# The low-rank gate of the third mixer: its first factor taken out of the weight stream

## The chip, the core and the metric

The kernel runs on one core of one Trainium2 chip. The metric is the device time of one launch in microseconds (us), lower is better. Three runs of the kernel before took 1793.9, 1794.4 and 1795.85 us; their median is 1794.4 us. A change of more than 0.2% (3.6 us) is about what a measurement of this kernel can tell from no change.

## What is computed

One layer of a hybrid decoder for 256 prompt tokens and 8 sampled tokens (264 columns together), everything in float32. One input projection `w_in` feeds three mixers; their outputs are projected, merged with gates, projected again, and an MLP follows. The part that the change touches is the third mixer (GLA), whose decay comes from a low-rank product: 2048 activations are first reduced to 16 numbers (`glr`) and then expanded to 512.

```python
h = rmsnorm(x, g_pre_mix) * (1.0 + sc1) + sh1
z = h @ w_in                       # 2048 x 15376
(z_uv, hq, hf, hi, hg, gq, gk, gv, gr, glr, z_gate) = split(z, offsets)
...
log_a = log_sigmoid(glr @ gla_w_up + gla_b_up) / GLA_TAU   # glr: 16 wide
o_g, S_g = gated_linear_recurrence(gq, gk * scale, gv, log_a, s_gla)
y_c = head_rmsnorm(o_g, gla_norm_g) * silu(gr)
merged = sum(gates[n] * (y_n @ w_branch[n]) for the three mixers)
out = merged @ w_out
```

## The kernel before

**The weight stream.** Almost all of the time goes into products of a weight matrix with the 264 activation columns. The activations are kept as two halves, `hh` and `hl` (a rounded part and the rest, blocks of [128, 4, 264]), and every weight is split in the same way: SP loads a raw item of [128 x 1024], ScalarE (ACT) casts each of its two halves to `whi` (`half_hi`, L667), VectorE (DVE) subtracts to get `wlo` (L671). One item makes one granule of 24 matmuls of 264 columns: for each 128 x 128 tile `whi` with `hh`, `whi` with `hl` and `wlo` with `hh`. `plan` lists the items in the order in which the granules come; items are loaded five ahead and split two ahead of the granule that uses them. `linear` and `zin` run the granules of one output tile and call `background()` after each.

**What runs beside it.** `background()` counts granules in `now` and advances the generators `mixer_a` and `mixer_r` (the three mixers) by a set rate per granule. These emit their small matmuls and transposes between granules, on PSUM tiles `sm` (three buffers), with their element-wise work on ACT and DVE. Some steps are held until a granule has passed (`READY`). `slot()` emits the matmuls of recurrence levels and of sampled states together with steps of the modulation weights (`ada`, float32, four groups of 32 columns of the array, L89, `Rounds.steps`).

**What sets the order.** In this part of the program the orders of PE and POOL are written out by hand: the instructions stand as the Python code emits them. ACT and DVE are given their work in the order that the scheduler of the language makes of it; each engine runs its list strictly in order.

**Where a mixer must be done.** The three branch products follow one another. At the start of the second (`branch(1, ...)`), `parts_b` calls `finish(0)` and `finish(1)`; `finish` calls `bg.drain`, which emits whatever is left of the mixer's generator at once, with no granule between. The last steps of a mixer are: eight matmuls for the outputs (`att`, L89), copies and squares on ACT (L1380, L1383), a reciprocal root on DVE (`rstd_small`, L249 to L255), eight scalings on ACT (L1389), and two sets of four transposes with their copies (L1400).

**The low-rank part.** `gla_group` allocates a block `wl`, zeroes it on POOL (L1141), loads the second factor `gla_w_up` into rows 0 to 15 of its first 512 columns (L1142), and runs `zin` over the columns of q and k. Then `z = zin(9216, P)` streams the first factor as an item 128 columns wide, of which 16 are used (two granules, 48 matmuls), and L1150 copies 16 rows of the sum to `lr`. After each tile of v one matmul with `wup` and `lr` gives 128 rows of the gate.

Of the kernel before, what the change touches and what calls it, by code (L numbers as in the profile page):

```python
# [7 lines left out]
F32 = mybir.dt.float32  # L8
# [7 lines left out]
P = 128  # L16
D = 2048
KT = D // P
NP = 256
NS = 8  # L20
NT = NP + NS
# [48 lines left out]
def hybrid_step_kernel(  # L70
# [8 lines left out]
    nc = tc.nc  # L79
    V, S = nc.vector, nc.scalar  # L80
# [23 lines left out]
    T = Products()  # L104
# [13 lines left out]
    def nm(s):  # L118
        uid[0] += 1
        return f"{s}_{uid[0]}"  # L120

    def blk(shape=None, dt=F32):
        shape = shape or [P, 4, NT]
        return blkp.tile(shape, dt, tag="b", name=nm("b"))

    def sm(shape=None):
        return psm.tile(shape or [P, 512], F32, tag="sm", name=nm("sm"))
# [10 lines left out]
    def add(o, a, b):  # L138
        V.tensor_tensor(o, a, b, op=ALU.add)  # L139
# [14 lines left out]
    def moving(v):  # L154
        return v.rearrange("p (r c) -> p c r", r=2)
# [43 lines left out]
    ps = sm()  # L199
# [121 lines left out]
    ps = sm([P, P])  # L321
# [184 lines left out]
    hh, hl = [], []  # L506
# [85 lines left out]
    def blocks(w, k0, nk, c0, width=CW):  # L592
        kc = min(nk, 1024 // width)
        return [(w, k0 + kb, kc, c0, width) for kb in range(0, nk, kc)]

    def plan():

        out, k0 = [], 0
        for n in CHUNKS:
            for gi in range(0, len(begin), 4 // n):  # L600
                out.append((win, k0, n, begin[gi][0], 4 // n * CW))
            k0 += n
        for c0 in (6144, 6400, 6656, 6912):
            out += blocks(win, 0, KT, c0)
        out += blocks(win, 0, KT, 9216, P)
        for s in range(4):
            out += blocks(win, 0, KT, 7168 + s * CW)
        for n in range(N_BRANCH):
            if n:
                g0 = 5120 if n == 1 else 8192  # L610
                for s in range(4):
                    out += blocks(win, 0, KT, g0 + s * CW)
            for m in range(8):
                out += blocks(win, 0, KT, 9232 + n * D + m * CW) + blocks(w_branch[0, n], 0, 8, m * CW)
        for m in range(8):
            out += blocks(w_out[0], 0, KT, m * CW)
        gap_at.append(len(out))
        for f in range(NFB + 1):
            if f < NFB:
                if f == 0:  # L620
                    out += blocks(w_mlp_up[0], 0, KT, 0, 2 * CW)
                for m in range(0 if f else 2, FB // CW):
                    out += blocks(w_mlp_up[0], 0, KT, f * FB + m * CW)
            if f:
                for m in range(8):
                    out += blocks(w_mlp_down[0], (f - 1) * (FB // P), FB // P, m * CW)
        return out
# [113 lines left out]
    def slot():  # L741

        lv = [x for x in levels if x[0] + AGE <= now[0]][:2]
        sv = [x for x in samples if x[0] + AGE <= now[0]]
        late = max([now[0] - x[0] for x in lv] + [0]) >= AGE + SLOT_WAIT + 3
        while lv and not T.room(LEVEL_N * len(lv) + 16 * len(sv)) and (len(lv) == 2 or not late):
            lv.pop()
        if lv or sv:
            T.short = T.spread(LEVEL_N * len(lv) + 16 * len(sv))
        del levels[:len(lv)]  # L750
        del samples[:len(sv)]
        if lv:
            pl = sm([P, 2, 8, 32])
            for i, (_, lhs, rhs, _) in enumerate(lv):
                for h in range(4):
                    for hf in range(2):
                        for b in range(4):
                            t0 = hf * P + b * 32
                            T.matmul(pl[32 * b:32 * b + 32, i, 2 * h + hf, :], lhs[:, h, t0:t0 + 32], rhs[:, h, t0:t0 + 32], start=True, stop=True)
        if sv:  # L760
            G, qm, os_ = sv[0][1]
            nh = 512 // G.dv
            po = sm([P, G.dv])
            for h in range(4):
                for i, (_, _, b, sts) in enumerate(sv):
                    T.matmul(po[32 * h:32 * h + 32, :], qm[:, h, b, :], sts[h // nh][:, h % nh, :], start=i == 0, stop=i == len(sv) - 1)
        if rounds.due():
            rounds.steps()
        for i, (_, _, _, put) in enumerate(lv):
            put(pl[:, i])  # L770
        if sv:
            if sv[0][2] == 0:
                V.tensor_copy(os_, po)
            else:
                add(os_, os_, po)
# [24 lines left out]
    def linear(w, k0, nk, c0, width, xh, xl):  # L800

        acc = new_acc()
        kc = min(nk, 1024 // width)
        for kb in range(0, nk, kc):
            granule(w, k0, kc, c0, width, [acc], xh, xl, kb, kb == 0, kb + kc == nk)
            background()
        return acc[:, 0:width // P, 0:NT]
# [4 lines left out]
    def pair(b, g):  # L812
        return b[:, 2 * g:2 * g + 2, :]
# [7 lines left out]
    win = w_in[0]  # L821

    def zin(c0, width=CW):
        return linear(win, 0, KT, c0, width, hH, hL)
# [26 lines left out]
    ]  # L851
    gap_at = []
    stream.append(Stream(plan()))
    stream[0].half_at = gap_at[0]
    first = First(0, CHUNKS[0])
# [224 lines left out]
    def log_sigmoid(out, z, a):  # L1080

        S.activation(a, z, AF.Abs)
        yield
        S.activation(a, a, AF.Exp, scale=-1.0)
        yield 1.6
        S.activation(a, a, AF.Ln, bias=1.0)
        yield 1.8
        V.scalar_tensor_tensor(out, z, 0.0, a, ALU.min, ALU.subtract)
        yield
# [45 lines left out]
    def gla_group():  # L1135
        G = Group()
        G.dv, G.i = 256, 2
        G.q, G.g, G.k, G.v = blk(), blk(), blk(), [blk(), blk()]
        wl = blk([P, 512 + NT])
        wup, lr = wl[:, 0:512], wl[:, 512:512 + NT]  # L1140
        nc.gpsimd.memset(wl, 0.0)  # L1141
        nc.gpsimd.dma_start(wup[0:16], gla_w_up[0])  # L1142
        for s in range(2):
            z = zin(6144 + s * CW)
            S.copy(pair(G.q, s), z)
        for s in range(2):
            z = zin(6656 + s * CW)
            S.activation(pair(G.k, s), z, AF.Copy, scale=GLA_SCALE)
        z = zin(9216, P)
        S.copy(lr[0:16], z[0:16, 0, :])  # L1150
        for s in range(4):
            z = zin(7168 + s * CW)
            S.copy(pair(G.v[s // 2], s % 2), z)
            ps = sm()
            T.matmul(ps[:, 0:NT], wup[:, s * P:(s + 1) * P], lr, start=True, stop=True)
            V.tensor_scalar(G.g[:, s, :], ps[:, 0:NT], bupT[:, s:s + 1], None, ALU.add)
        G.s_in = lambda b, h, n: state_gla[0, b, h:h + n].rearrange("h k v -> k h v")
        G.s_out = lambda b, h, n: gla_sample[0, b, h:h + n].rearrange("h k v -> k h v")
        G.p_out = lambda h, n: gla_prompt[0, 0, h:h + n].rearrange("h k v -> k h v")

        def gates():
            yield from log_sigmoid(G.g, G.g, blk())
            V.tensor_scalar(G.g, G.g, 1.0 / GLA_TAU, None, ALU.mult)
            yield

        G.gates = gates
        return G
# [251 lines left out]
    rate[:] = RATES[0]  # L1419
    rounds.gap = 2  # L1420
    Gs.append(gla_group())
    gens.append(mixer_r(Gs[2]))
    bg.g.append(gens[2])
# [162 lines left out]
    for m in range(8):  # L1586
# [4 lines left out]
        z = linear(w_out[0], 0, KT, m * CW, CW, mH, mL)  # L1591
# [37 lines left out]
    ps = sm([P, 2, KT, NS])  # L1629
# [197 lines left out]
    pt, ps = sm([P, 2, CW]), sm([P, 2 + NS])  # L1827
# [20 lines left out]
    def put(eng, t, hf, c0):  # L1848
        eng.dma_start(y_prompt[0, t * P:(t + 1) * P, hf * 1024 + c0:hf * 1024 + c0 + 512], piece(yt, t, hf, c0))
# [16 lines left out]
    ps = sm([P, P])  # L1866
# [63 lines left out]
```

## Time and profile before

| what | value |
|---|---|
| three runs | 1793.9, 1794.4, 1795.85 us |
| the profiled execution, its span | 1792.8 us (no time of its own is given beside it; the median of the runs is 1.6 us above) |
| busy: weight loads of PE, DVE, ACT, POOL | 94%, 66%, 56%, 8% |
| read from HBM | 427.60 MB, 245 GB/s over the span with what is written |
| the q tiles of the third mixer are copied (L1145) | 298.2 and 309.5 us |
| the low-rank sum is copied (L1150) | 347.2 us |

The span is the time from the first to the last instruction of one profiled execution. PE is the matmul engine; its weight loads overlap its matmuls and are listed as PEld. The chain of the profile is the work that ended last, followed back from the last instruction; a matmul group in it carries its time on PE. Matmuls are pipelined, so the duration of a single one (277 ns for a 264-column one) is longer than the distance from one to the next. A float32 matmul of the program stands in the trace as two records.

### The profile page before, as it was taken

To read this page: it belongs to the slowest core of one execution; us is meant where nothing else is said; L and a number is where in the kernel's file an instruction comes from. 1 tells how busy PE (TensorE), PEld (TensorE's weight loads), DVE (VectorE), ACT (ScalarE), POOL (GpSimd) and SP (SyncE) were. 2 spreads that over 40 slices of the span, in tenths; PEclk is the share of its full clock that TensorE was granted. 3 is DMA by queue.
4 is the path that set the end of the run, shared out by engine and by line. 5 is a ranking of instruction groups with operands and counts; after the bars stand their busy time and mean duration, and the time that the engine had idled before them with its cause. 6 is when DMAs were issued, how large, how long until landed. Compare 5 with 4: busy or idle time off the path is not lost.

```text
span 1792.8 us, 42113 instructions
## 1 busy us (share of the span) xinstructions
PE 1770.3 (99%) x16970; PEld 1686.2 (94%) x16970; DVE 1183.8 (66%) x2079; ACT 1002.5 (56%) x1823; POOL 140.5 (8%) x228
## 2 busy tenths in 40 slices
PE   6999999999999999999999999999999999999998
PEld 5899999989999999899999989999999999999997
DVE  5676668697588697466566666645666666666666
ACT  5444554666766766655455665555454545454544
POOL 4222000101102012110000010000000000000000
PEclk9999999999999999999999999999999999999999
DMA  9998597789699789898866946776666666666663
GB/s 343 392 354 296 184 340 249 227 293 309 208 290 320 236 285 311 286 370 264 266 193 206 319 140 220 239 254 204 193 196 198 194 197 195 194 199 192 198 191 117
DMA packets 330179, 442.05 MB, mean 247 GB/s; under 512 B 14946, under 2 KB 276944, under 8 KB 329984
## 3 DMA queue, kind: packets, MB, share of 16 engines
q1 hardware_dynamic: 312160, 381.05, 65.5%
q0 software_dynamic: 17184, 57.85, 9.2%
q8 instruction: 133, 2.18, 0.5%
q14 instruction: 62, 0.51, 0.1%
q10 hardware_dynamic: 640, 0.47, 0.1%
HBM read 427.60 MB, written 11.70 MB: 245 GB/s over the span
## 4 chain that ended last, share of the span: by engine, by line
PE 95%; DMA 2%; DVE 2%; ACT 1%; issue 0%; SPq 0%; DVEq 0%; ACTq 0%
PE mm L89 86%; PE ada L89 5%; PE sm L89 3%; PE sm L93 1%; DMA b<-in_w_ada_dram 1%; DVE wlo L671 1%; DMA b<-in_x_prompt_dram 0%; DVE b L139 0%; DVE b L1670 0%; DVE b L142 0%; ACT b L1356 0%; ACT b L145 0%; SPq L532 0%; SPq L186 0%; DVE b L136 0%
## 5 line engine op out<-in xcount | busy, mean ns | idle before, releaser
L89 PE MATMUL mm<-b,whi 128*128 128x264 f32 x9248 | 1578.8, 277 | 1.3 <-DVE b L920 0.4
L89 PEld LDWEIGHTS mm<-b,whi 128*128 128x128 f32 x9248 | 1394.4, 189 | 35.0 <-issue 19.9
L89 PE MATMUL mm<-b,wlo 128*128 128x264 f32 x4624 | 1275.5, 276 | 0.0
L671 DVE TENSOR_TENSOR wlo<-raw,whi 128x512 fp32r<-128x512 f32 x1118 | 760.3, 690 | 462.1 <-ACT whi L667 459.2
L667 ACT CAST whi<-raw 128x512 fp32r<-128x512 f32 x1118 | 681.7, 617 | 620.2 <-DVE wlo L671 315.6
L89 PEld LDWEIGHTS mm<-b,wlo 128*128 128x128 f32 x4624 | 873.5, 189 | 0.2
L139 DVE TENSOR_TENSOR b<-b,mm 128x528 f32<-128x528 f32 (+1 forms) x137 | 95.7, 699 | 55.6 <-PE mm L89 49.0
L89 PE MATMUL ada<-b,cT 128*32 128x256 f32 (+2 forms) x888 | 66.2, 421 | 3.4 <-DMA b<-in_w_ada_dram 3.1
L89 PEld LDWEIGHTS ada<-b,cT 128*32 128x32 f32 x888 | 26.1, 112 | 34.1 <-issue 17.2
L1860 POOL TENSOR_TENSOR gs<-b,G 128x16 f32<-128x16 f32 x1 | 0.2, 222 | 714.1 <-DVE b L139 714.1
L532 POOL DMA_DIRECT2D b<-in_w_ada_dram x64 | 46.3, 726 | 44.1 <-PE ada L89 35.1
L1214 POOL DMA_DIRECT2D out_dram<-st x32 | 23.5, 735 | 234.0 <-DVE st L1213 227.6
L667 ACT CAST whi<-araw 128x512 fp32r<-128x512 f32 x38 | 23.1, 618 | 26.2 <-PE mm L89 22.0
L89 PE MATMUL ada<-araw,cT 128*32 128x512 f32 x264 | 35.6, 599 | 0.0
L1211 ACT ACTIVATE st<-st,fs 128x128 f32<-128x128 f32 (+1 forms) x96 | 35.2, 426 | 0.0
L136 DVE TENSOR_TENSOR b<-b,b 128x512 f32<-128x512 f32 (+1 forms) x47 | 34.4, 747 | 1.2 <-ACT b L1325 0.8
L1213 DVE SCALAR_TENSOR_TENSOR st<-vbc,b,st 128x128 f32<-128x128 f32 (+1 forms) x96 | 32.4, 392 | 1.2 <-ACT st L1211 1.2
L93 PE MATMUL sm<-cst,b 128*128 128x128 f32 (+1 forms) x149 | 21.5, 285 | 8.2 <-DMA b<-in_g_post_mix_dram 5.0
L671 DVE TENSOR_TENSOR wlo<-araw,whi 128x512 fp32r<-128x512 f32 x38 | 24.6, 686 | 5.3 <-ACT whi L667 5.3
L93 PEld LDWEIGHTS sm<-cst,b 128*128 128x128 f32 (+1 forms) x149 | 17.5, 147 | 9.2 <-issue 6.0
L142 DVE TENSOR_TENSOR b<-b 128x1024 f32<-128x1024 f32 (+1 forms) x24 | 24.4, 1022 | 1.5 <-PE ada L89 1.4
L142 DVE TENSOR_TENSOR b<-gt,b 128x528 fp32r<-128x528 f32 x32 | 22.7, 709 | 3.6 <-ACT whi L667 0.5
(303 smaller groups left out, 819.5 us busy)
## 6 DMA issues: line engine op xcount, KB each, us to landing
raw<-in_w_in_dram SPq DMA_DIRECT2D x225, 512.0 KB, 5.2
raw<-in_w_mlp_down_dram SPq DMA_DIRECT2D x128, 512.0 KB, 3.6
raw<-in_w_mlp_up_dram SPq DMA_DIRECT2D x125, 512.0 KB, 3.9
araw<-in_w_ada_dram SPq DMA_DIRECT2D x66, 512.0 KB, 6.1
b<-in_w_ada_dram SPq DMA_DIRECT2D x62, 512.0 KB, 6.8
b<-in_w_ada_dram POOLq DMA_DIRECT2D x48, 512.0 KB, 9.6
raw<-in_w_branch_dram SPq DMA_DIRECT2D x48, 512.0 KB, 4.7
raw<-in_w_out_dram SPq DMA_DIRECT2D x32, 512.0 KB, 4.5
```

What stands on the lines that cost most here:

```text
L89: return nc.tensor.matmul(out, w, x, **kw)
L93: return nc.tensor.transpose(*a)
L136: V.tensor_tensor(o, a, b, op=ALU.mult)
L139: V.tensor_tensor(o, a, b, op=ALU.add)
L142: V.tensor_tensor(o, a, b, op=ALU.subtract)
L532: queue.dma_start(w[:, i], w1[k * P:(k + 1) * P, :, self.k0 * P:(self.k0 + self.n) * P])
L667: self.last = [S.copy(hi, raw).ins, None]
L671: self.last[1] = V.tensor_tensor(lo, raw, hi.bitcast(F32), op=ALU.subtract).ins
L1211: S.activation(st[:, i, :], st[:, i, :], AF.Copy, scale=fs[:, h0 + i, b:b + 1])
L1213: V.scalar_tensor_tensor(st[:, i, :], v[:, i, :], k[:, h0 + i, NP + b:NP + b + 1], st[:, i, :], ALU.mult, ALU.add)
L1214: nc.gpsimd.dma_start(G.s_out(b, h0, nh), st)
L1860: Q.tensor_tensor(gs[:, 14:16, :], dst[:, :, NP:NT], G2[:, 14:16, 1:NC], op=ALU.mult)
```

## The change

The first factor is no longer an item of the stream: the line in `plan` goes, and with it two items, their loads, four casts, four subtractions, two granules and their two calls of `background()`. Its 16 columns are loaded once by a POOL DMA straight into the second half of `wl`, as [128, 16, 32] with 16 of every 32 columns filled, and `gla_w_up` is loaded four times, at rows 0, 32, 64 and 96. A new function `low_rank` calls `slot()` and then emits 32 float32 matmuls of 32 x 264: for each block of four k tiles, and for both halves of the activations, four matmuls on four groups of 32 columns of the array. Their sums lie in four groups of 32 rows of one `sm` tile; they are copied whole (128 rows) to `lr`, which is now the last quarter of `G.g`, and the second product adds the four groups up by its contraction over 128 rows.

```diff
@@ plan
-        out += blocks(win, 0, KT, 9216, P)
@@ gla_group
-        wl = blk([P, 512 + NT])
-        wup, lr = wl[:, 0:512], wl[:, 512:512 + NT]
+        wl = blk([P, 1024])
+        wup, wlr = wl[:, 0:512], wl[:, 512:1024].rearrange("p (k c) -> p k c", k=KT)
         nc.gpsimd.memset(wl, 0.0)
-        nc.gpsimd.dma_start(wup[0:16], gla_w_up[0])
+        nc.gpsimd.dma_start(wlr[:, :, 0:16], win[:, 9216:9232].rearrange("(k p) c -> p k c", p=P))
+        for j in range(4):
+            nc.gpsimd.dma_start(wup[32 * j:32 * j + 16], gla_w_up[0])
+        lr = G.g[:, 3, :]
+
+        def low_rank():
+
+            slot()
+            ps = sm()
+            for s in range(4):
+                for i, x in enumerate((hh, hl)):
+                    for j in range(4):
+                        T.matmul(ps[32 * j:32 * j + 32, 0:NT], wlr[:, 4 * s + j, :], moving(x[s].bitcast(F32)[:, j, :]),
+                                 start=s == 0 and i == 0, stop=s == 3 and i == 1)
+            S.copy(lr, ps[:, 0:NT])
...
-        z = zin(9216, P)
-        S.copy(lr[0:16], z[0:16, 0, :])
+        low_rank()
```

**First place: PE at the low-rank product.** `mm` are the tiles of the stream, `sm` the small tiles; the two sets of transposes belong to the first HGRN mixer. Before, PE goes on with the stream (mm_4635 is the low-rank tile):

```order
L89 MATMUL mm_4454<-b_2720,wlo_4484 128x264
L93 MATMUL sm_4620<-cst,b_178 128x128 x4
L93 MATMUL sm_4627<-cst,b_178 128x128 x4
L89 MATMUL mm_4635<-b_331,whi_4521 128x264
L89 MATMUL mm_4635<-b_332,whi_4521 128x264
```

and with the change:

```order
L93 MATMUL sm_4624<-cst,b_178 128x128 x4
L93 MATMUL sm_4631<-cst,b_178 128x128 x4
L89 MATMUL sm_4639<-b_331,b_3876 32x264 x4
L89 MATMUL sm_4639<-b_332,b_3876 32x264 x4
L89 MATMUL sm_4639<-b_1254,b_3876 32x264 x4
L89 MATMUL sm_4639<-b_1255,b_3876 32x264 x4
L89 MATMUL sm_4639<-b_1993,b_3876 32x264 x4
L89 MATMUL sm_4639<-b_1994,b_3876 32x264 x4
L89 MATMUL sm_4639<-b_2720,b_3876 32x264 x4
L89 MATMUL sm_4639<-b_2721,b_3876 32x264 x4
L89 MATMUL mm_4673<-b_331,whi_4525 128x264
```

The 48 stream matmuls of the low-rank tile are gone, and 32 float32 matmuls stand directly behind the transposes; the next tile of the stream is the first v tile.

**Second place: PE and ACT at the start of the second branch.** The tiles `os` hold the sampled outputs of the two HGRN mixers; the transposes of b_8563 (before) or b_8631 (now) are the last ones of the second HGRN mixer. Before, they stand 96 stream matmuls (mm_8637) behind the mixer's last output products:

```order
L89 MATMUL mm_8637<-b_2720,wlo_8667 128x264
L93 MATMUL sm_8819<-cst,b_8563 128x128 x4
L93 MATMUL sm_8825<-cst,b_8563 128x128 x4
L93 MATMUL sm_8833<-cst,b_3874 128x128 x4
L93 MATMUL sm_8840<-cst,os_915_5285 128x128
L93 MATMUL sm_8844<-cst,os_1247_7431 128x128
L89 MATMUL mm_8856<-b_331,whi_8701 128x264
```

Now they stand 48 (the second half of mm_8576) behind them, and after the first `os` transpose, that is in the drain of `finish(1)`:

```order
L89 MATMUL mm_8576<-b_2720,wlo_8606 128x264
L93 MATMUL sm_8789<-cst,os_915_5354 128x128
L93 MATMUL sm_8798<-cst,b_8631 128x128 x4
L93 MATMUL sm_8804<-cst,b_8631 128x128 x4
L93 MATMUL sm_8810<-cst,os_1243_7436 128x128
L89 MATMUL mm_8822<-b_331,whi_8669 128x264
```

On ACT the eight scalings (L1389 before, L1402 now) that these transposes read stood, before, ahead of four casts and of the activation of the gate tile mm_8637:

```order
L1389 ACTIVATE b_8563<-b_8563,rr_8561 128x128 x2
L667 CAST whi_8705<-raw_8541 128x512
L1389 ACTIVATE b_8563<-b_8563,rr_8561 128x128 x2
L667 CAST whi_8770<-raw_8601 128x512
L667 CAST whi_8774<-raw_8601 128x512
L667 CAST whi_8808<-raw_8670 128x512
L667 CAST whi_8812<-raw_8670 128x512
L1468 ACTIVATE b_8020<-mm_8637 128x528
L1400 COPY b_8818<-sm_8819 128x2x256
```

Now the last four stand behind the activation of that gate tile (mm_8576), with the copy of the transposes next:

```order
L666 CAST whi_8760<-raw_8609 128x512
L1402 ACTIVATE b_8631<-b_8631,rr_8629 128x128 x3
L666 CAST whi_8764<-raw_8609 128x512
L1402 ACTIVATE b_8631<-b_8631,rr_8629 128x128
L1481 ACTIVATE b_7972<-mm_8576 128x528
L1402 ACTIVATE b_8631<-b_8631,rr_8629 128x128 x4
L1413 COPY b_8797<-sm_8798 128x2x256
```

Two granules of cover between the mixer's last products and its transposes are gone, the two that the low-rank tile had.

**Third place: POOL ahead of the third mixer's tiles.** Before:

```order
L480 TENSOR_TENSOR b_533<-xsn_132,A_169 128x2x8
L481 TENSOR_TENSOR b_533<-b_533,mod 128x2x8
L1141 MEMSET b_3876 128x776
L1142 DMA b_3876<-in_gla_w_up_dram 16x512
L1051 DMA out_dram<-sqs_4425 64x128
```

and now:

```order
L480 TENSOR_TENSOR b_533<-xsn_132,A_169 128x2x8
L481 TENSOR_TENSOR b_533<-b_533,mod 128x2x8
L1140 MEMSET b_3876 128x1024
L1141 DMA b_3876<-in_w_in_dram 128x16x16
L1143 DMA b_3876<-in_gla_w_up_dram 16x512 x4
L1050 DMA out_dram<-sqs_4429 64x128
```

POOL issues five DMAs where it issued one, and the first of them gathers 2048 pieces of 16 numbers (64 bytes).

## The prediction

> **What bounds the kernel now.** I read the page first, then the waits of PE, then single stretches of the timeline where the change acts.
>
> ```profile
> span 1792.8 us, 42113 instructions
> PE 1770.3 (99%) x16970; PEld 1686.2 (94%) x16970; DVE 1183.8 (66%) x2079; ACT 1002.5 (56%) x1823; POOL 140.5 (8%) x228
> PEclk9999999999999999999999999999999999999999
> PE 95%; DMA 2%; DVE 2%; ACT 1%; issue 0%; SPq 0%; DVEq 0%; ACTq 0%
> PE mm L89 86%; PE ada L89 5%; PE sm L89 3%; PE sm L93 1%; DMA b<-in_w_ada_dram 1%; DVE wlo L671 1%; DMA b<-in_x_prompt_dram 0%; DVE b L139 0%; DVE b L1670 0%; DVE b L142 0%; ACT b L1356 0%; ACT b L145 0%; SPq L532 0%; SPq L186 0%; DVE b L136 0%
> ```
>
> PE is busy in 99% of the span at a full clock, and 95% of the chain that ended last is PE's, 86% the stream's matmuls. So a change is worth what it adds to or takes from PE's own list, plus the waits that it opens or closes in it. In the mixers' part (200 to 900 us) the waits of PE (in total, times, longest) are these alone:
>
> ```profile
> PE sm L89 <- DVE vsb L139: 0.6, 1, 0.6
> PE sm L93 <- ACT b L1400: 0.4, 2, 0.3
> ```
>
> PE waits there for no half of a weight and no DMA. The work that the change takes from SP, ACT and DVE (two items, four casts, four subtractions) therefore buys nothing by itself: PE hides it now, and would still.
>
> **What is removed from PE.** The low-rank tile in the chain, with the transposes ahead of it (start, us, what):
>
> ```profile
> 337.68 0.87 PE sm L93 x8
> 338.55 5.40 PE mm L89 x48
> ```
>
> Its 48 matmuls take **5.40 us** of PE, 0.1125 each. All of that goes.
>
> **What is added to PE.** 32 float32 matmuls of 32 x 264. The nearest rows are the modulation products, float32 on the same four groups of columns: one stretch from the chain, and two groups of the view by form (count | busy us, mean ns).
>
> ```profile
> 115.34 3.59 PE ada L89 x64
> L89 PE MATMUL ada<-b,cT 128*32 128x256 f32 x384 | 22.4, 381 | 0.0
> L89 PE MATMUL sm<-b,b 128*128 128x256 f32 x24 | 6.3, 383 | 0.1
> ```
>
> A float32 matmul leaves two records, so the 64 records are 32 matmuls of 256 columns, eight groups of four: 3.59 / 8 = 0.449 us a group. The last row has 12 full-width matmuls of the same length in 6.3 us, 0.52 each at most: the four of a group run beside each other. At 264 columns the eight groups take 3.59 x 264/256 = **3.70 us**; with 0.1 for the change of shape behind the transposes I take +3.8. Bounds: 3.6 (the row as it is), and 32 x 0.52 = 17 us if nothing ran side by side, which the first row excludes for this form.
>
> The Trainium skill, "TensorE: Matmul & The Clock Gate", section "Measured speedup vs the span model", gives less for packing: 3.07 times for four row tiles, 2.38 for three column tiles. By 3.07 a group would be 4 x 0.52/3.07 = 0.68 us and the product 5.6 instead of 3.7. This trace does not agree, 0.449 for a group of four, so the row stands.
>
> **Returns to the stream.** In the order of PE the stream is cut into 123 stretches instead of 117, since the small batches fall otherwise. In the chain a stretch of 48 takes 5.40 or, with a start from another shape, 5.60:
>
> ```profile
> 388.56 5.60 PE mm L89 x48
> 396.62 5.40 PE mm L89 x48
> ```
>
> So six more cost 0 to 1.2 us; I take **+0.5**, as the small batches that now stand alone were elsewhere in longer ones and their number of matmuls is the same.
>
> **The drain at the second branch.** The mixers advance by granules, and two granules are gone. The second HGRN mixer has to be done at a fixed place, and the order shows its last transposes 48 stream matmuls behind its last output products instead of 96. Before, that stretch ran so (PE, then ACT, then DVE; start, us):
>
> ```profile
> 601.55 0.39 PE L89 MATMUL sm<-b,att 128*128 128x128 f32 x2
> 601.87 0.66 PE L89 MATMUL sm<-st,b 128*32 128x128 f32 x16
> 614.23 1.47 PE L93 MATMUL sm<-cst,b 128*128 128x128 f32 x12
> 615.97 0.33 PE L93 MATMUL sm<-cst,os 128*128 128x128 f32 x1 [0.27 <-ACT b L1400]
> 616.46 0.33 PE L93 MATMUL sm<-cst,os 128*128 128x128 f32 x1 [0.16 <-ACT b L1400]
> 616.54 0.47 PE L89 MATMUL mm<-b,whi 128*128 128x264 f32 x2
> ```
>
> ```profile
> 604.14 0.31 ACT L1383 ACTIVATE vt<-b 128x128 f32<-128x128 f32 x1
> 607.31 1.28 ACT L1389 ACTIVATE b<-b,rr 128x128 f32<-128x128 f32 x4 [0.48 <-DVE rr L255]
> 610.40 0.69 ACT L1389 ACTIVATE b<-b,rr 128x128 f32<-128x128 f32 x2
> 614.84 0.61 ACT L1468 ACTIVATE b<-mm 128x528 f32<-128x528 f32 x1
> ```
>
> ```profile
> 604.57 0.17 DVE L249 TENSOR_SCALAR sx<-ss 128x8 f32<-128x8 f32 x1 [1.63 <-ACT vt L1383]
> 607.11 0.17 DVE L255 SCALAR_TENSOR_TENSOR rr<-sa,rr 128x8 f32<-128x8 f32 x1
> ```
>
> The output products end at 601.87. The last square is read off about 604.5, the reciprocal root is there at 607.3, the last scaling ends at 611.1: a chain of **9.2 us** on ACT and DVE. PE came to the transposes at 614.23, 12.4 behind the products, 3.1 after the scalings were done. Now it comes 5.5 us behind them (48 matmuls, no modulation step between), transposes one `os` tile (0.1) and would be through both sets (eight transposes; above, x8 took 0.87) at 6.5. With the chain at 9.2 and the last set of four (0.4) behind it, it is through at 9.6: a new wait of **3.1 us**. Queued behind it on PE stands everything, the stream included; on ACT the gate's activation (0.5) now stands ahead of the last four scalings, about what the scaling and square of the `os` tile took there before, so I leave 9.2. Bounds: 0, if ACT and DVE get through in time, and 3.6, if the second set adds its copies.
>
> One wait goes at the same place. Before, 14 transposes stood in a row on three buffers, with the copies L1400 behind that activation: from 614.23 to 616.54, 2.3 us for what at 0.11 each (0.87 for 8) is 1.4 to 1.5. Now four of them (the third mixer's first) come later, behind 72 stream matmuls: **-0.9**.
>
> What is late next: `yparts` of this branch has the 96 matmuls of the first gate tile (10.8 us) as cover, before and now.
>
> **The gather.** 2048 pieces of 64 bytes, and three more copies of `gla_w_up`, start about 245 us, where the DMA engines are full and PE takes a modulation step whose weights have just landed:
>
> ```profile
> 244.83 0.56 POOL L1142 DMA_DIRECT2D b<-in_gla_w_up_dram  x1 [0.29 <-POOL b L1141]
> 322.15 0.58 POOL L1051 DMA_DIRECT2D out_dram<-sqs  x1 [76.76 <-ACT sqs L1050]
> 245.00:265.00 20.00, 20.00 (x177) 18.44 (x178) 13.48 (x25) 11.36 (x19) 0.39 (x1) 1.00 1.03 366
> q1 hardware_dynamic: 312160, 381.05, 65.5%
> q0 software_dynamic: 17184, 57.85, 9.2%
> L376 SPq DMA_DIRECT2D b<-in_w_ada_dram x2: 382/419/456, 254.1 to 254.7; - x2
> DMA to landing us min/median/max: 5.5/5.9/6.2
> 262.11 1.04 PE L89 MATMUL ada<-b,cT 128*32 128x512 f32 x8
> ```
>
> The second of these loads is issued at 254.7 and lands 6.2 later, 260.9; PE uses it at 262.11: 1.2 us of slack. From shares of 16 engines' span: q1's packets of 1.22 KB take 60 ns, q0's of 3.37 KB 154 ns, a line with 44 ns a KB and 7 ns fixed, so 10 ns for 64 bytes: 2048 x 10/16 = 1.3 us of all engines, and 0.3 for the 96 KB of copies. Past the slack that is **+0.3** (an estimate from the two rows). Bounds: 0, and 60 ns a piece (q1's), 7.7 us, past the slack 6.8. I take the line, since both rows lie on bytes far more than on packets. The gather itself has until 338 and hides behind 90 us of stream; POOL's next work stands at 322, so a longer memset and four more issues there cost nothing.
>
> **ACT at the low-rank copy.** The copy to `lr` now stands directly behind two copies of transposes, so ACT waits for PE about as long as the product lasts, with the casts and the first mixer's gate queued behind it. PE takes 3.8 for the same product without using a half, and two granules are split ahead: no loss, as long as the halves are not later than before.
>
> **The sum.** -5.4 + 3.8 + 0.5 + 3.1 - 0.9 + 0.3 = **+1.4 us** on the span of 1792.8, so 1794.2; the median of the runs stands 1.6 above that span, so 1795.8.
>
> **The rivals.**
>
> *No wait in the drain.* If the chain of scalings is done in time, the 3.1 goes: 1792.7, a small gain. For it: the two HGRN mixers use the same steps, and ACT has gaps. Against it: 9.2 us are measured, 5.5 are left, and ACT's order puts four scalings behind the gate tile's end.
>
> *Slower: the small pieces hold up the loads.* Place: the modulation weights at 261 us. It starts to cost above 7 ns a piece (1.2 us of slack less 0.3 of copies), and passes the 0.2% above about 27. At a price as for 512 bytes on the line, 7 + 22 = 29 ns, the loads come 3.8 + 0.3 late, PE waits 2.9 instead of 0.3: 1798.4. At 60 ns a piece, 1802.3. For it: the DMA share is 1.03 there. Against it: 64 bytes are little, and other halves have more room. The Trainium skill, "DMA: Bandwidth & Descriptors", section "Specifications", has 512 B as the least transfer for line rate, with a read-modify-write below it; by that rule this rival holds, and no run here shows it yet.
>
> *The change does not do what it says:* the four groups of columns run one after another. 17 instead of 3.8: 1809. The 3.59 us row is against it.
>
> *Halves late at the first mixer's gate,* if ACT's wait pushes casts: about 1 us, 1796.8.
>
> **How the numbers follow.** Forecast 0.60 (its own range 1794.6 to 1797.0, by the bounds of the returns, the wait and the gather); no wait 0.20; small pieces 0.12; one after another 0.03; halves late 0.05. The range, 1792.4 to 1799.0, takes in the no-wait case and the lower price of the small pieces. Within 0.2% (about what a measurement can tell from no change) is 1790.8 to 1798.0: forecast, no wait and late halves lie in it, 0.83 with the edges taken off; slower 0.14 from the small pieces and the serial case; faster 0.03, if returns and wait both come to nothing.
>
> **What would show it.** Right: the 32 matmuls in 3.7 to 3.9 us behind the transposes; PE waiting some 3 us for ACT's scalings at the transposes of the second branch, and no wait for L1400's counterpart; 123 stretches of the stream; about 0.3 us of wait at the modulation step of 262 us. Wrong: a low-rank product far over 4 us, PE idle on casts or DMAs behind it, or the second branch's transposes passing without a wait; then the time is that of the rival named.

## The result and the profile after

| | before | after |
|---|---|---|
| median | 1794.5 us (1792.6 to 1795.85, 9 runs) | 1797.7 us (1795.9 to 1802.25, 9 runs) |
| ratio after to before | | 1.0025, 95% interval 1.0017 to 1.0033 |
| the profiled execution | span 1792.8 us | 1796.8 us, span 1795.0 us |

The changed kernel is slower: 3.2 us by the medians (0.18%), 0.25% by the ratio, whose interval is clear of 1. That lies in the range on record, 1.9 us above the forecast. The 0.2% lies inside the interval, so on which side of it the change falls is not settled. The first lines of the page of the changed kernel read as before, PE still being the bound:

```profile
span 1795.0 us, 42158 instructions
PE 1772.2 (99%) x16986; PEld 1683.7 (94%) x16986; DVE 1181.6 (66%) x2079; ACT 999.4 (56%) x1819; POOL 142.8 (8%) x232
PE 95%; DVE 2%; DMA 2%; ACT 1%; issue 0%; SPq 0%; DVEq 0%; ACTq 0%
```

The two spans differ by 2.2 us only, because the profiled execution of the changed kernel came to the first stream matmul 1.4 us earlier (25.86 against 27.25 us), on a stretch that the change doesn't touch. From that matmul to the end of PE's list it took **3.55 us** more. Cutting PE's list of both traces at every start of a matmul, and giving each piece to the matmul that opens it, says where:

| piece of PE's list | before | after | difference |
|---|---|---|---|
| stream matmuls at 0.1125 each (13872, 13824) | 1560.6 | 1555.2 | -5.4 |
| what the stretches of the stream (117, 123) take beyond that | 20.8 | 22.5 | +1.7 |
| the low-rank product | | 4.61 | +4.61 |
| transposes of the mixers and of `os` | 14.5 | 17.2 | +2.7 |
| the rest | | | -0.1 |

The 1.7 has two parts. Six more stretches at a mean of 0.15 (before's stretches, all but the seven dearest, are 110 and take 16.1 us beyond their matmuls) are 0.9; the other 0.75 stand in a single stretch, that of 616 us, at the second branch. The waits of PE between 200 and 900 us, of the changed kernel (in total, times, longest), name the place:

```profile
PE sm L93 <- ACT b L1402: 2.3, 2, 1.9
PE sm L89 <- DVE vsb L139: 0.6, 1, 0.6
```

The drain at the second branch, in PE's timeline of the changed kernel (the output products end at 606.2; the first row is the end of the 48 matmuls behind them), and with ACT's timeline of the same stretch below:

```profile
611.54 0.28 PE L89 MATMUL mm<-b,wlo 128*128 128x264 f32 x1
611.65 0.27 PE L93 MATMUL sm<-cst,os 128*128 128x128 f32 x1
612.35 0.33 PE L93 MATMUL sm<-cst,b 128*128 128x128 f32 x1 [0.42 <-ACT b L1402]
614.53 1.76 PE L93 MATMUL sm<-cst,b 128*128 128x128 f32 x7 [1.85 <-ACT b L1402]
616.08 0.42 PE L93 MATMUL sm<-cst,os 128*128 128x128 f32 x1
616.15 0.79 PE L89 MATMUL mm<-b,whi 128*128 128x264 f32 x2
```

```profile
611.89 0.99 ACT L1402 ACTIVATE b<-b,rr 128x128 f32<-128x128 f32 x3 [0.88 <-DVE rr L255]
613.29 0.40 ACT L1402 ACTIVATE b<-b,rr 128x128 f32<-128x128 f32 x1
613.59 0.59 ACT L1481 ACTIVATE b<-mm 128x528 f32<-128x528 f32 x1
614.08 1.27 ACT L1402 ACTIVATE b<-b,rr 128x128 f32<-128x128 f32 x4
```

PE stands idle for 0.42 and 1.85 us with one transpose between. The eight scalings are through at 615.35, 9.2 us behind the products. The second wait ends with the fifth scaling, which stands behind the gate's activation (L1481). Then something shows that the prediction does not have: seven transposes take 1.55 us from their start to the next piece, 0.22 each, where eight took 0.87 before. The windows of the changed kernel around it (from:to, length, PE, PEld, DVE, ACT and POOL busy, granted clock, DMA share, GB/s) show what goes with it:

```profile
611.60:614.50 2.90, 0.65 (x4) 0.24 (x3) 2.83 (x7) 2.61 (x8) 0.00 (x0) 0.98 0.62 181
614.50:618.00 3.50, 3.47 (x17) 3.48 (x18) 1.91 (x4) 3.09 (x6) 0.00 (x0) 0.53 0.53 150
618.00:625.00 7.00, 7.00 (x64) 7.00 (x64) 5.66 (x8) 4.11 (x6) 0.00 (x0) 1.00 0.24 65
```

The granted clock is 0.53 for the 3.5 us behind the wait, and 1.00 again after it. A wait of 2.3 us is paid there a second time: in the transposes (1.55 instead of 0.76), in part hidden by scalings that were late anyhow, and in the first six matmuls of the stream, which stand 0.22 apart instead of 0.11. Whether the idle time is what lowers the clock is tested below.

And the low-rank product, in the chain of the changed kernel (start, us, what), where the prediction had 3.8:

```profile
336.09 0.87 PE sm L93 x8
336.96 4.61 PE sm L89 x63
341.57 5.49 PE mm L89 x47
```

### The profile page after: what moved, and what is told of

It reads as the page before. It is cut to its first block, busy times and chain, and to the rows that moved or that the text cites. A ratio compares the mean times of both kernels' runs of the same rounds, so it can differ in the third digit from the quotient of the medians.

```text
span 1795.0 us, 42158 instructions
## 1 busy us (share of the span) xinstructions
PE 1772.2 (99%) x16986; PEld 1683.7 (94%) x16986; DVE 1181.6 (66%) x2079; ACT 999.4 (56%) x1819; POOL 142.8 (8%) x232
## 4 chain that ended last, share of the span: by engine, by line
PE 95%; DVE 2%; DMA 2%; ACT 1%; issue 0%; SPq 0%; DVEq 0%; ACTq 0%
PE mm L89 85%; PE ada L89 5%; PE sm L89 4%; PE sm L93 1%; DMA b<-in_w_ada_dram 1%; DVE wlo L670 1%; DMA b<-in_x_prompt_dram 0%; DMA raw<-in_w_in_dram 0%; DVE b L139 0%; DVE b L1683 0%; SPq L532 0%; ACT b L1402 0%; DVE b L142 0%; ACT whi L666 0%; SPq L186 0%
## 5 line engine op out<-in xcount | busy, mean ns | idle before, releaser
L139 DVE TENSOR_TENSOR b<-b,mm 128x528 f32<-128x528 f32 (+1 forms) x137 | 95.7, 699 | 56.1 <-PE mm L89 49.6
L666 ACT CAST whi<-araw 128x512 fp32r<-128x512 f32 x38 | 23.1, 618 | 26.0 <-PE mm L89 22.5
L89 PE MATMUL sm<-b,b 128*32 128x32 f32 (+4 forms) x392 | 30.1, 275 | 0.1
L89 PEld LDWEIGHTS sm<-b,b 128*32 128x32 f32 (+1 forms) x392 | 22.3, 138 | 4.4 <-issue 1.2
```

Source lines behind the costliest of these rows:

```text
L89: return nc.tensor.matmul(out, w, x, **kw)
L666: self.last = [S.copy(hi, raw).ins, None]
```

## The experiments

**Theory.** The slowdown is the drain, which two lost calls of `background()` make, and the product is dearer than predicted because of something in how it reads. **Rivals.** The loss comes from the product and from its copy on ACT; the product has a fixed price per group; the gather takes part.

### The two calls and the product, apart

Put the two calls back behind the product (e1):

```diff
         low_rank()
+        background()
+        background()
```

> The changed kernel with two calls of background() put back behind low_rank(), so the mixers stand two granules further on, as before. Theory (the drain at the second branch is the loss: PE idle behind the scalings, then half the granted clock, 3.5 us together, plus six more returns to the stream at 0.15 each, 0.9): no wait for L1402's scalings at the transposes of the second branch, 117 stretches, and about 4.3 us less than the changed kernel, so 1793 to 1794, within 0.1% of before. Rival (the loss lies in the product itself and in what it pushes on ACT): the wait stays, 1797 to 1798. A second rival (the two calls in a row only move the crowding to the low-rank place): a new wait of PE near 340 us.

And the other way round: leave the low-rank tile in the stream of the kernel before, and drop its two calls only (e3).

```diff
-        z = zin(9216, P)
+        acc = new_acc()
+        for kb in range(0, KT, 8):
+            granule(win, 0, 8, 9216, P, [acc], hH, hL, kb, kb == 0, kb + 8 == KT)
+        z = acc[:, 0:1, 0:NT]
```

> The kernel before, with the low-rank tile in the stream as it was, but without the two calls of background() after its two granules. Theory (the lost calls alone make the drain): a wait of 2 to 3 us for the scalings at the second branch's transposes, half the granted clock for some 3 us behind it, 123 or 124 stretches, and 4 to 4.5 us more than before, about 1798.8. Rival (the drain comes from the product, for instance from the later copy to lr): 1794.5, no wait.

Medians, with the kernel before (29 runs) on the same chip, and the changed kernel from the measurement above:

| | two calls | no calls |
|---|---|---|
| low-rank tile in the stream | 1794.3 (before) | 1798.4, ratio 1.0024 [1.0013, 1.0034] |
| column-group product | 1794.65, ratio 1.0003 [0.9994, 1.0012] | 1797.7, ratio 1.0025 [1.0017, 1.0033] |

The loss goes with the calls, not with the product: without the calls +4.1 with the tile in the stream and +3.0 with the product; +0.4 by the product alone. With the calls back, PE's timeline at the second branch (e1) is that of before, row for row, and no row waits more than 0.27 for L1415, the copies of the transposes (L1413 in the changed kernel, L1400 before):

```profile
614.67 1.47 PE L93 MATMUL sm<-cst,b 128*128 128x128 f32 x12
616.42 0.33 PE L93 MATMUL sm<-cst,os 128*128 128x128 f32 x1 [0.27 <-ACT b L1415]
616.91 0.33 PE L93 MATMUL sm<-cst,os 128*128 128x128 f32 x1 [0.16 <-ACT b L1415]
```

Without the calls, but with the tile in the stream (e3), the scalings (L1392 there) are waited for as in the changed kernel, and the clock falls in the same way. First its waits of PE, then its windows:

```profile
PE sm L93 <- ACT b L1392: 2.3, 2, 1.9
```

```profile
613.00:615.90 2.90, 0.65 (x4) 0.24 (x3) 2.83 (x7) 2.61 (x8) 0.00 (x0) 0.94 0.57 181
615.90:619.40 3.50, 3.47 (x18) 3.47 (x19) 1.91 (x4) 3.11 (x6) 0.00 (x0) 0.56 0.56 150
```

The stretches of the stream count 117 with the calls and 124 without. So theory holds for the drain and for the returns. The second rival of the first run, a new wait near 340 us, is out too: e1 has none there. Its 1793 to 1794 was missed by 0.65 us: the product took 4.61 as in the changed kernel, so with the 48 matmuls gone (5.4) PE's list should be 0.8 shorter than before's, and the median is 0.4 above, with an interval of 1.6 us on either side. The list of its one profiled execution is 1.5 us longer than before's, not 0.8 shorter; 1.8 us of the gap are modulation steps, which take more time there (2.45 us instead of 1.85 for the one at 260 us). What the product saves by itself is too small to be seen in the medians.

### How the product reads its columns

The halves lie with the even tokens first and the odd ones behind them, 132 columns on; `moving` reads from the two places in turn. Read in the order in which they lie, with the order undone in the copy (e2):

```diff
-                        T.matmul(ps[32 * j:32 * j + 32, 0:NT], wlr[:, 4 * s + j, :], moving(x[s].bitcast(F32)[:, j, :]),
+                        T.matmul(ps[32 * j:32 * j + 32, 0:NT], wlr[:, 4 * s + j, :], x[s].bitcast(F32)[:, j, :],
...
-            S.copy(lr, ps[:, 0:NT])
+            S.copy(lr.rearrange("p (c r) -> p r c", r=2), ps[:, 0:NT].rearrange("p (r c) -> p r c", r=2))
```

> The changed kernel, but the float32 product reads its moving columns in the order in which they lie, and the copy to lr undoes the order. Theory (reading two columns 132 elements apart is what makes a pass of four groups 0.288 us instead of 0.231): the 64 records take 3.7 us instead of 4.61, and the time falls by 0.9 to about 1796.8. Rival (the surplus is a fixed price per group of four, such as its weight loads): 4.6 as before and the same time, 1797.7.

And every second column, then the others (e11):

```diff
-                        T.matmul(ps[32 * j:32 * j + 32, 0:NT], wlr[:, 4 * s + j, :], moving(x[s].bitcast(F32)[:, j, :]),
+                        T.matmul(ps[32 * j:32 * j + 32, 0:NT], wlr[:, 4 * s + j, :], x[s].bitcast(F32)[:, j, :].rearrange("p (c r) -> p r c", r=2),
...
-            S.copy(lr, ps[:, 0:NT])
+            S.copy(lr.rearrange("p (c b a) -> p a c b", a=2, b=2), ps[:, 0:NT].rearrange("p (b a c) -> p a c b", a=2, b=2))
```

> The changed kernel with the product's moving columns read two apart (every second column, then the others) instead of from two places 132 columns apart in turn. Theory (any distance between neighbours slows the four column groups): the 64 records take 4.6 us. Rival (only the jump between two far places does): 3.7. The time of the whole is not looked at.

The product in the chains of the two kernels, in order first, then every second:

```profile
337.01 3.70 PE sm L89 x64
```

```profile
336.98 3.90 PE sm L89 x62
```

The time runs to the next piece of the chain, also where it lists fewer than the 64 records. 3.70 us in order, which is the prediction's term to the digit; 3.90 with every second, so near the rival and not the theory of that run; 4.61 from two far places. For one of the 16 passes of four groups that is 0.231, 0.244 and 0.288 us. So the surplus is the reading, and most of it the jump between the two places; a fixed price per group is out. The Trainium skill, "SBUF — State Buffer", section "Door 1: The DMA port swizzle", has a rule for this: memory is read in lines of 16 bytes, two or more accesses to a line in a row are free, and each step to a new line costs. By it four columns of float32 in a row are free, every second one (two a line) just so, and two places in turn (one a line) not. The three prices stand in that order, and the trace agrees, but for the 0.2 us of the middle case. That the lines are the cause, no run here tests. The stream's own matmuls read the same halves in the same jumps at 0.1125 us each; no run here shows whether they pay for it.

The time as a whole didn't show the 0.9: e2's median is 1797.6, ratio 1.0016 [1.0007, 1.0025] (e11 was run once, for its trace; its time comes up under what stays open).

### The gather

The DMA of the first factor, issued four times, that is this line three times more (e4):

```diff
+        nc.gpsimd.dma_start(wlr[:, :, 0:16], win[:, 9216:9232].rearrange("(k p) c -> p k c", p=P))
```

> The changed kernel with the gather of 2048 pieces of 64 bytes issued four times over. Theory (a piece costs the DMA engines little enough that the loads' slack takes it): the same as the changed kernel, within 1 us, no wait at the modulation steps near 262 us. Rival at 10 ns a piece on each of 16 engines: three more gathers are 3.9 us of all engines, a wait of 2 to 3 us there. At 29 ns a piece: 11 us more.

1797.7 us, ratio 1.0024 [1.0015, 1.0034]: the changed kernel's time. POOL's timeline of this run shows what was tested (start, us, and what ended the idle time):

```profile
245.56 1.20 POOL L1141 DMA_DIRECT2D b<-in_w_in_dram  x1 [0.29 <-POOL b L1140]
251.04 1.15 POOL L1142 DMA_DIRECT2D b<-in_w_in_dram  x1 [4.28 <-DMA b<-in_w_in_dram]
258.67 1.15 POOL L1143 DMA_DIRECT2D b<-in_w_in_dram  x1 [6.48 <-DMA b<-in_w_in_dram]
266.43 1.15 POOL L1144 DMA_DIRECT2D b<-in_w_in_dram  x1 [6.61 <-DMA b<-in_w_in_dram]
```

Each waits for the one before (by up to 6.6 us); they write the same place. So this is not four at once but a gather under way through all of 246 to 274 us. Three more gathers cost nothing that the medians show, where 29 ns a piece would have been 11 us.

What the first one costs is less clear. The modulation step at 260 us, from its start to the next piece of PE's list, takes 1.85 us in both traces without the gather (before and e3). In the eleven traces with it, it takes 1.85 (the changed kernel) to 3.09 us (e8), with a mean of 2.44. In e4, where a second gather has landed by then and a third is under way, it takes 2.34, no more than with one. So nothing grows with the number of pieces, and 10 ns a piece does not fit. But the step is longer in ten of the eleven, 0.6 us as a mean of them all. Two traces without a gather are few, and no run takes out the gather alone, so whether it is the cause stays open.

### The clock behind the wait

24 transposes of the identity into a tile that nobody reads, ahead of the last transposes of the second HGRN mixer (e5):

```diff
+        if G.i == 1:
+            fill = sm()
+            for _ in range(24):
+                T.transpose(fill[:, 0:P], ident, ident)
```

> The changed kernel with 24 transposes of the identity, which nobody reads, ahead of the last transposes of the second HGRN mixer, so that PE works through the 2.3 us in which it waits for the scalings. Theory (the clock falls because PE stood idle): the granted clock stays at 1.0 between 612 and 618 us, the eight transposes take 0.9 and the stretch behind them 0.1 over its 8.1, so 1.4 to 1.6 us less than the changed kernel: 1796.1. Rival (the low clock there has another cause): 0.5 again behind the filler, and the same 1797.7 or more.

PE's timeline of this run at the place, then its windows:

```profile
612.36 2.78 PE L93 MATMUL sm<-cst 128*128 128x128 f32 x24
614.98 1.35 PE L93 MATMUL sm<-cst,b 128*128 128x128 f32 x8
616.16 0.27 PE L93 MATMUL sm<-cst,os 128*128 128x128 f32 x1
```

```profile
611.60:614.50 2.90, 2.90 (x29) 2.90 (x28) 2.73 (x9) 2.02 (x7) 0.00 (x0) 1.00 0.53 178
614.50:618.00 3.50, 3.50 (x31) 3.12 (x30) 2.46 (x5) 3.50 (x9) 0.00 (x0) 1.00 0.48 140
```

The granted clock stays at 1.00 when PE has work: in the changed kernel it falls because PE is idle. From the end of the 48 matmuls to the stream it takes 3.94 us instead of 4.50, and the stretch behind it 8.18 instead of 8.99: 1.37 us less, a little under the 1.4 to 1.6 expected, since the last scalings are still waited for (1.19 for eight transposes). The median is 1797.07, ratio 1.0019 [1.001, 1.0028], 0.6 below the changed kernel's, so the trace settles this and the medians don't.

### Putting it together, and going further

The calls and the reading in order, together (e6):

```diff
-                        T.matmul(ps[32 * j:32 * j + 32, 0:NT], wlr[:, 4 * s + j, :], moving(x[s].bitcast(F32)[:, j, :]),
+                        T.matmul(ps[32 * j:32 * j + 32, 0:NT], wlr[:, 4 * s + j, :], x[s].bitcast(F32)[:, j, :],
...
         low_rank()
+        background()
+        background()
```

> The changed kernel with the two calls of background() put back and the moving columns of the product read in order. If the two effects add, 64 records in 3.70 us, no wait at the second branch, 117 stretches: 0.9 less than with the calls alone (1794.65), so 1793.7, and 0.5 us under before. If the shorter product only shifts a wait to ACT's copies or to the halves behind it: 1794.6.

1792.7 us, ratio to before 0.9993 [0.9984, 1.0001]. Measured again (e10):

> The kernel with the two calls and the reading in order, measured again with the others of this call. If the first measurement (1792.7, ratio 0.9993) was no chance: 1792 to 1794 and under before. If it was a good draw of the first 250 us, which vary by 1.5 us from run to run: 1794.3 like before.

1793.8 us, ratio 0.9998 [0.9989, 1.0007]. All 22 runs have a median of 1793.2, against 1794.3 and 1794.0 for the kernel before in the two sets. It beats the changed kernel by 4.5 us; against the kernel before it is some 1 us less, which the intervals don't hold apart from no change. By its terms PE's list should be 1.7 us shorter than before's (3.7 instead of 5.4). In the two profiled executions it is 0.6 and 0.1 us longer; modulation steps account for 1.7 and 0.5 us of the gap, and in the second run a wait that the profile doesn't name for another 0.5.

Three steps beyond it did not pay. Four calls instead of two (e8):

```diff
         low_rank()
-        background()
-        background()
+        for _ in range(4):
+            background()
```

> As the kernel with both edits, but with four calls of background() at the product instead of two, so the mixers are two granules ahead of where they stood before. Theory (the lead at the second branch is what prices the transposes there): the last transposes of the second HGRN mixer come before the drain, the waits of before for L1400 (0.4 and the stretched transposes) go as well, and 113 stretches instead of 117: 1.0 to 1.5 us less than with two calls, 1792.4. Rival (a lead beyond that of before buys nothing, or the pumped steps crowd at 340 us): 1793.7 or more.

The last transposes came before the drain, with 113 stretches and no wait for their copies, but PE waited 1.3 us for nothing that the profile names ("issue", at 672 us), and the median is 1794.3, ratio 0.9999 [0.9991, 1.0008]. Then 16 matmuls on the sum of the halves, added by POOL (e7):

```diff
+        hs = [blk() for _ in range(4)]
+        for s in range(4):
+            nc.gpsimd.tensor_tensor(hs[s], hh[s].bitcast(F32), hl[s].bitcast(F32), op=ALU.add)
...
-                for i, x in enumerate((hh, hl)):
-                    for j in range(4):
+                for j in range(4):
+                    T.matmul(ps[32 * j:32 * j + 32, 0:NT], wlr[:, 4 * s + j, :], hs[s][:, j, :], start=s == 0, stop=s == 3)
```

> As the kernel with both edits, and POOL first adds the two halves of the activations into four blocks, so that the product takes 16 float32 matmuls instead of 32. Theory (the product is priced by its passes, 0.231 us each): 32 records in 1.85 us, so another 1.85 us less, 1791.9, if the four blocks held for 90 us delay nothing. Rival (blocks are short, or POOL's additions slow DVE): a wait of PE between 250 and 340 us, and 1793.7 or more.

And 20 matmuls, with three blocks added by DVE into blocks that are free until later (e9):

```diff
+        hs = [G.v[0], G.v[1], G.g]
+        def whole(s):
+            V.tensor_tensor(hs[s], hh[s].bitcast(F32), hl[s].bitcast(F32), op=ALU.add)
...
+            xs = [(0, hs[0]), (1, hs[1]), (2, hs[2]), (3, hh[3].bitcast(F32)), (3, hl[3].bitcast(F32))]
```

> As the kernel with the two calls and the reading in order, with three of the four blocks of activations summed from their halves by DVE (into the v blocks and the gate's block, which are free until then), so the product takes 20 float32 matmuls instead of 32. Theory (the product is priced by passes; no block is held and POOL is left out): 40 records in 2.3 us, 1.4 less: 1791.3. Rival (DVE's three additions make the low halves of the weights late): a wait of PE on wlo between 290 and 330 us, and 1792.7 or more.

Both products came out at their price by passes, in the chains of the two kernels, POOL's sums first:

```profile
344.68 1.92 PE sm L89 x32
```

```profile
343.49 2.37 PE sm L89 x40
```

Both kernels lost more elsewhere: 1797.6, ratio 1.002 [1.0011, 1.0029], and 1796.1, ratio 1.0012 [1.0003, 1.0021]. The waits of PE between 200 and 900 us, POOL's sums first, then DVE's:

```profile
PE mm L89 <- ACT b L1160: 3.9, 1, 3.9
PE mm L89 <- DVE b L139: 1.4, 3, 1.0
```

```profile
PE sm L89 <- DVE vsb L139: 3.4, 1, 3.4
```

With four more blocks held, the copy of a q tile (L1160) is late and with it the stream's next tile; that blocks are what it lacks wasn't tried apart. The longest of the waits for L139 (1.0 us, at 269.7) has another source. While POOL makes two of its sums (263.09 to 268.37 us), two subtractions of DVE take 4.66 us, and the next one 0.68; the addition that PE waits for stands behind those two. POOL's timeline, then DVE's:

```profile
263.09 5.28 POOL L1147 TENSOR_TENSOR b<-b,b 128x1056 f32<-128x1056 f32 x2 [13.60 <-PE ada L89]
```

```profile
264.26 4.66 DVE L670 TENSOR_TENSOR wlo<-raw,whi 128x512 fp32r<-128x512 f32 x2 [1.75 <-ACT whi L666]
269.45 0.68 DVE L670 TENSOR_TENSOR wlo<-raw,whi 128x512 fp32r<-128x512 f32 x1
```

That half of the run's rival is what the trace shows. With DVE's sums it is the first mixer's statistics that come late (0.6 in the kernel before, in the changed one and with the calls put back), and the clock falls behind that wait as well.

## Why the prediction came out as it did

**What was right.** The forecast had the mechanism and the sign of the sum, on its span and in the median: the product takes the place of the 48 matmuls at nearly their price, and the two lost calls bring the drain to within 48 matmuls of the products. The chain of scalings was put at 9.2 us and took 9.2 (606.2 to 615.35). PE was to be through with the transposes at 9.6 behind the products, and was at 9.9 (616.08). No wait for L1413, the counterpart of L1400, 123 stretches, no wait behind the low-rank copy: as forecast.

**What was mis-sized,** against the +1.4 of the sum:

| term | predicted | measured |
|---|---|---|
| 48 matmuls removed | -5.4 | -5.4 |
| low-rank product | +3.8 | +4.6; 3.70 in order (e2) |
| six more returns | +0.5 | +0.9 (at 0.15 each) |
| the drain, less the wait that goes | +3.1 - 0.9 | +2.7 in the transposes, +0.75 in the stream behind them |
| gather | +0.3 | 0 in this trace |
| sum | +1.4 | +3.55 |

- *The product.* The step that failed was taking the row of the modulation products over to this one: they have the same form, but their moving operand lies in one piece, and that of `low_rank` comes from two places in turn. The upper bound (17 us, nothing side by side) was no help, since it bounds another failure. The Trainium skill's 3.07 ("TensorE: Matmul & The Clock Gate", "Measured speedup vs the span model"), which the prediction set aside, would have given 5.6; the measured 3.70 stands by the row.
- *The returns.* Between the bounds of 0 and 1.2 I took the middle. A return costs 0.15 us as a mean over all but the dearest stretches, which the trace of before shows already; the bound was nearer than the value.
- *The drain.* The wait was right (2.3 us of it shows as idle). What I left out is that PE runs at half its granted clock after it, for 3.4 us. With PE kept at work (e5) the same place takes 1.37 less, and 3.45 less 1.37 is 2.1, about the 2.2 of the sum. The trace of before shows this nowhere in the mixers' part, since its waits there are 0.6 us and less. Of the Trainium skill's page "TensorE: Matmul & The Clock Gate", I used the packing and not Part 1, which says that the clock is halved after an idle window of some 3.4 us and comes back after some 3.4 us of work. The trace agrees with the second and differs from the first: a wait of 2.3 us was enough here. By half a clock over 3.4 us, an estimate, the term would have been up to 1.7 larger, and the forecast 1797.5.
- *The gather.* The 0.3 was an estimate from rows of larger packets. In the trace of after the step at 260 us takes 1.85 us, as before, so the wait of 0.3 that was to be seen there is not; ten other traces with the gather have 0.06 to 1.24 more at that step. So the term is neither borne out nor refuted.

**The rivals.** No wait in the drain: refuted by the waits, 2.3 us. Small pieces that hold up the loads, at 29 ns a piece or more: refuted by e4. One group after another: refuted by the 4.61. Halves late at the first mixer's gate: no such wait in the trace of after. Within 0.2% had 0.83 and slower 0.14; the ratio's interval holds the 1.002, in its lower half. What happened is the forecast's own case, 0.7 beyond its own range of 1794.6 to 1797.0, and none of the cases that I had given to the slower side. That the time still lies inside the range on record is in part luck: its upper end, 1799.0, was there for the small pieces, which did not come about.

**What stays open.** The changed kernel's nine runs spread more (6.4 us) than those of the kernel before (3.3 us) in the same set; two lie at 1801.7 and 1802.25, and no trace of this kernel shows such a run. The one execution of e11, which differs from it in the reading of the product alone, took 1800.9 and gives a hint. From the first stream matmul on, PE's list is 4.1 us longer than in the trace of after. A load of modulation weights comes 1.9 us late, and the clock falls behind that wait too (PE's timeline, then the windows):

```profile
427.88 1.76 PE L89 MATMUL ada<-araw,cT 128*32 128x512 f32 x4 [1.93 <-DMA araw<-in_w_ada_dram]
```

```profile
428.00:431.50 3.50, 3.50 (x13) 1.95 (x12) 0.00 (x0) 0.00 (x0) 0.00 (x0) 0.51 0.93 314
431.50:434.00 2.50, 2.50 (x24) 2.50 (x24) 0.69 (x1) 1.17 (x3) 0.00 (x0) 1.00 0.95 333
```

## What to carry to other kernels

Work that is taken out of a stream also takes out the ticks by which other work is paced: ask what else was hung on each iteration, and give it its ticks back. A wait on the engine that bounds the kernel can cost more than its length, because the clock falls behind it; price it at its length plus up to half of the time for which the clock stays low behind it (3.4 us behind most waits here, 5.4 behind that of e9). And a row is a price for a new operation only if the operands lie in memory in the same way.

## What the hardware showed

- The granted clock follows idle time closely. Idle 0.42 and 1.85 us with one transpose between: half the clock for 3.4 us. Idle 1.93 us at a stretch (e11, above): half as well, for as long. Idle 3.9 us (e7): the same, as the last three windows of it below show. Idle 1.0 us (e7, at 268 us) and 1.3 us (e8, at 672 us) left it at 1.00. So in these traces the line for a single idle stretch lies between 1.3 and 1.9 us; whether it moves, they don't tell.

```profile
268.40:269.70 1.30, 0.29 (x4) 0.12 (x2) 1.30 (x3) 0.00 (x0) 0.00 (x0) 1.00 0.87 356
269.70:271.00 1.30, 1.30 (x12) 1.30 (x13) 1.30 (x3) 0.00 (x0) 0.00 (x0) 1.00 0.78 199
309.90:314.20 4.30, 0.38 (x4) 0.18 (x2) 4.14 (x6) 1.34 (x3) 0.00 (x0) 0.99 0.63 184
314.20:317.50 3.30, 3.30 (x15) 3.30 (x16) 0.00 (x0) 0.88 (x2) 0.00 (x0) 0.50 0.79 248
317.50:319.00 1.50, 1.50 (x15) 1.50 (x14) 0.81 (x2) 0.41 (x2) 0.00 (x0) 1.00 0.08 29
```

- The low clock can last longer: in e9 PE waits from 314.2 to 317.6 us, and the clock is at half for 6.8 us from 316.2 on, so for 5.4 us of work.

```profile
316.00:323.00 7.00, 5.42 (x25) 5.43 (x25) 4.90 (x25) 0.62 (x1) 0.00 (x0) 0.51 0.54 150
323.00:326.00 3.00, 3.00 (x28) 3.00 (x28) 1.77 (x5) 1.24 (x2) 0.00 (x0) 1.00 0.09 12
```

- Transposes count as work for the clock: 24 of them in the wait kept it at 1.00 (e5).
- A float32 pass on four groups of 32 columns costs 0.231, 0.244 or 0.288 us for 264 columns, by whether its columns are read in a row, every second, or from two places 528 bytes apart in turn.
- Beside additions of POOL (128 x 1056, float32, two operands each) two subtractions of DVE (128 x 512) took 4.66 us, and one behind them 0.68 (e7).
